# Token tiles in shared PSUM banks, and the low parts of the samples made by VectorE, in a hybrid decoder layer

## The chip, the cores and the metric

The kernel runs on one core of a Trainium2 chip. The metric is device time in microseconds (us) of one execution. Before the change it took 1491.72 us, the median of 3 runs (1490.73 to 1493.11).

In the profile PE is TensorE (matmuls), PEld its weight loads, DVE is VectorE, ACT is ScalarE, POOL is GpSimd, and SP (SyncE) issues the DMAs. L554 is line 554 of the kernel's file.

## The reference, cut to what matters

One inference step of a one-layer decoder, for a prompt of 1024 tokens and for 64 sample tokens (8 sequences of 8) that share the weights. The change touches the first stage only: the norm of the tokens, and the columns v and gmlp_v of the first projection.

```python
def rmsnorm(x, g):
    y = x * rsqrt(mean(x * x, axis=-1, keepdims=True) + EPS)
    return y * g

h = rmsnorm(x, norm_mix)                           # (tokens, 1024)
q, k, v, gu, gv, ga, gb = split_in(h @ w_in)
o = attention(q, k, v)                             # window of 128, per-head sinks
vn = layernorm(gelu(gv), ln_g, ln_b)
s = gelu(gu) * (tril(w_s) @ vn + b_s)              # inside chunks of 128 positions
merged = sigmoid(ga) * (o @ w_pa) + sigmoid(gb) * (s @ w_pb)
x = x + merged @ w_out
x = x + conv_ffn(rmsnorm(x, norm_ffn))             # up, conv of width 3, gelu gate, down
y = rmsnorm(x, norm_final)
```

All is in float32. The kernel splits each float32 factor into a high part (a rounding that TensorE multiplies in one pass) and a low part (what is left), and adds three products: high by high, high by low and low by high.

## The kernel before, in words

**Tiling of the first stage.** The tokens are in two groups. Group 0 has 576: the 64 samples ("s") and four tiles of 128 prompt tokens. Group 1 has four tiles of 128. The 1024 channels are 8 chunks of 128, numbered k. For v and gmlp_v the tokens are the stationary operand and 256 columns of weights the moving one, so that one token tile takes 8 chunks by 3 products = 24 matmuls of 128x256, and the sample tile 16: its high and low parts stand side by side in one array of 128 columns (`both` in `h_of`), so that high and low are multiplied by one matmul with the high weights and one with the low.

**The start.** For each chunk k of group 0 the tile `x` is loaded, and `h_of` makes the parts: ACT the high part of all 576 tokens (L536), DVE the low part of the 512 prompt tokens (L538, one scalar-tensor-tensor), and POOL the low part of the 64 samples in two instructions (L542, L543) by way of a tile `hx`. PE multiplies the chunk as it comes into five accumulators (`ps5`, one PSUM bank for each token tile; L554 is the matmul of `mm_tok`). Between these, ACT squares each chunk in place (L648), DVE adds the eight squares up (`rsg[0]`, L650, 128x576 each), and the weights are split too (L40 and L41; `w2h`, `w2l`). `stats_tok` (L494 to L501) then sums the squares over the channels on PE (tile `mx`), and ACT and DVE make 1/rms of it (`rst`). No accumulator can be taken out before that, since each is scaled by `rst`.

**The token sets.** `tokens(g, key, out, ...)` runs one set: all token tiles of a group by 256 columns. The sets are, in order: gv 1, v, gv 2 on group 0 (5 tiles each); v, gv 2, gv 0, gv 1 on group 1 (4 tiles each). gv 0 on group 0 is the start above. Each tile's matmuls go into a bank of its own, from the pool `psa` of seven (tag `st`). `out` takes it out: ACT scales it by `rst` (L569 for v, L596 with the gelu for gv), for the samples after ACT has copied one half of the partitions (L561) and DVE has added the other (L562, tile `gs`). In between, ACT and DVE also do jobs for group 1: its x (L44, L45, L665 to L668), and sums of the T0 tiles.

**What sets the order.** Each engine works through its instructions strictly in the order of a table, `ORDER`, by which `issue_order` rearranges what the code above emits. Semaphores between engines, and waits for a buffer that is to be used again, are put in by the framework.

Of the kernel before, what the change touches and what calls it, by code (L numbers as in the profile page):

```python
# [6 lines left out]
F32 = mybir.dt.float32  # L7
# [3 lines left out]
ALU = mybir.AluOpType  # L11
# [23 lines left out]
def layer(tc, a):  # L35
    nc = tc.nc
    V, S, G, PE = nc.vector, nc.scalar, nc.gpsimd, nc.tensor
# [5 lines left out]
    def scale_split(hi, lo, src, by):  # L43
        S.activation(hi, src, AF.Copy, scale=by)  # L44
        V.scalar_tensor_tensor(lo, src, by, hi.bitcast(F32), ALU.mult, ALU.subtract)  # L45

    with ExitStack() as top:
# [209 lines left out]
        def right(stack, name, bufs=1):  # L257
            return stack.enter_context(tc.tile_pool(name=name, bufs=bufs, side="right", reuse_waits="tile"))
# [122 lines left out]
        with ExitStack() as ph1:  # L381
# [109 lines left out]
            def bank():  # L491
                return psa.tile([P, 512], F32, name="st")
# [28 lines left out]
            hp0 = right(hs0o, "hs0")  # L521
# [3 lines left out]
            def h_of(g, k, x):  # L525
                n = groups[g]["n"]
                by = gains[:, 0, k:k + 1]
                if g:
                    hh, hl = (hp1.tile([P, n], F32R, name=f"h{y}{k}") for y in "hl")
                    scale_split(hh, hl, x, by)  # L530
                    hs[g].append((hh, hl, None))
                    return
                both = hp0.tile([P, 2 * n], F32R, name=f"h{k}")
                hh, hl = both[:, n:], both[:, 0:n - NS]
                for lo, hi in ((0, 320), (320, n)) if k == 0 else ((0, n),):
                    S.activation(hh[:, lo:hi], x[:, lo:hi], AF.Copy, scale=by)  # L536
# [493 lines left out]
            def acc2():  # L1030
                return pmm.tile([P, 1024], F32, name="mm")
# [420 lines left out]
            hx = {}  # L1452
# [247 lines left out]
        with ExitStack() as ph3:  # L1700
# [109 lines left out]
            bank = [psd.tile([P, 512], F32, name="dn") for _ in range(6)]  # L1810
# [90 lines left out]
def issue_order(tc):  # L1901
# [8 lines left out]
    for name, text in ORDER.items():  # L1910
# [14 lines left out]
DIGITS = "0123456789abcdefghijklmnopqrstuvwxyzABCDEFGHIJKLMNOPQRSTUVWXYZ"  # L1925
ORDER = {
    "Pool": (
        "(67)66(7)22..24..6(4)2..24..6(4)2..24..6(4)2..2(8)24..4..4..4..4..4..4..4..4..4..4..4..4(14)ff(4"
        ")1..11.2(4)22(4)2213.2..1(5)6d3..2...3..2...63.b.2...3..2...63..2.8a..3..2..21(4)7.3..2...63.b.2"
        "...3..2...63.b.2...3..2...3.b4.52..2(5)3.4.2.8..3..2...63.b.2...3..2...63.b.2...3..2...6..533.2."  # L1930
        "21"
# [17 lines left out]
        ".3.3(9)2j2i4.35e1466a.9.88.71(8)11121..14l13514g62.466aaaaa.91.1.1...1(5)1(5)1...1.1...1"  # L1949
    ),  # L1950
    "DVE": (
        "..nn2(6)91..1.44..2.1...1.1(6)123..3(4)1..1.1.1..26.1.31.2..2g.ff2.dd1ck.jj.iii...777cc.bd.c.b2a"
        ".9388.87.62.222(4)2.2.33.22g.1(6)e.e.cccficc(6)66a(5)3.5.235f..3.e45..4..468.1.51..3..192.23.7.3"
        "5..5.1(5)15..35[126]6[125][130]2[129]5.37h[130]..[138]5[136].g8[124](4)46(4)2449..26f.h...66(4)4"
        "47..49.3h.6i.9(5)46(4)2449..26fi(4)66(4)447..47.3d.4e.51..24..254e55555yyyy.4w4v.24dg22.2.1..249"
        "6b.1..22.13c3.d..2..2496b.31..1213.7a22..32546.3a.3b.2.13.6274a..47il..58...7.9.e.9.b..1b.ka.9.."
        "1h.7.8(4)6b8d(4)68hk(4)46..6.7.98.7..5.94.3..7.5..1423.23.11.1.3522.4723341.1(4)11(6)L1..227(4)4"
        "...11112.11122(6)1111...2x(4)22(4)J3.21.211.222..1.2N..11(4)2.221.11.2522..11N3312121.2..11(4)2R"
        "..11.11.2(4)22..222..1.2F..112.1.2.22(10)2.1.222...e.11...q(6)F(4)2(4)4332..151M33112.1333...161"
        "54T1..262143...1..3227..1..322N..151.32..1.4.22O..262.43...11433...1..222t..26254(4)151438h111.1"  # L1960
        "1(4)1b.22d.11...2.b...23e2.9.3..714.73.5.b4..55b.44..587..3..5.1.4.1.3.5...2.2413..31.131.2.3.7."
        ".d..633.1.14..2..11.3.1.33552262x24.22...u.25.16.244..3(5)12.2.24578957672755234.344757496.88871"
        "365..11(4)2262c5c.a3f9..g.6..46(4)2g5g..ddim...aa(4)8..6.f..6..aa.f9i..7...46(4)2g5g..ddim...aa("
        "4)8..6.f..6..aa.f9i..7...46(4)2g5g..ddhj...aa...8.7..4.4.2.7..5..3.2(5)11.4.e3.cc1h.aaah(4)8..6."
        "f..6..aa.f9i...6..46(4)2g5g..ddim...aa(4)8..6.f..6..aa.f9i..7...46(4)2g5g..ddim...aa(4)8..6.f..6"
        "..aa.e9f...6.5..4.3...1b.bag.9..7.6..6.5.2.14.a3ca..7.6ae.5.6(4)25fg..ddim...aa(4)8..6.f..6..aa."
        "f9i..7...46(4)2g5g..ddim...aa(4)8..6.f..6..aa.f9i..7...46(4)2g5g..ddim...aa(4)8..6.b..6..66.55.."
        ".b2a..1133.3.2(6)1322.1..7..4..2.1.1(8)1(4)51.1(9)1..11.11.11.11.11...11.a.8..1.4.[75]3.1..11.[6"
        "7][69].[68][70]..11.[65](7)7(6)2b.b.b8..1..6(5)23.3.3.3.3.3.b.b.b8b(5)3(4)23.3.3.3(9)88.7...77.1"
        "2...11.1..3..11..11(10)21311111...88(4)4a4...a..118.111.11.111...41.1.2(5)2..3.32..1"  # L1970
    ),
    "SP": (
        "(6)1(17)6789(4)7...3.2.a.ach(10)7.e.d.3d.c.1o(5)99.aa...948..625(4)33.23f.e..511(7)1(13)21.5(4)1"
# [109 lines left out]
```

## Time and profile before

| what | value |
|---|---|
| median of 3 runs | 1491.72 us |
| the profiled execution's own time | 1490.81 us |
| its span in the profile | 1489.1 us |
| PE busy in the span | 1480.2 us (99%) |
| DVE, ACT, POOL busy | 1181.0, 856.9, 286.6 us |
| granted TensorE clock, mean | 0.999 |
| matmuls of the first stage (L554) | up to 107.2 us of the span |
| share of the chain that ended last that is PE | 93% |

The span runs from the first to the last instruction; 1.7 us of the execution's time lie around it. A matmul's duration overlaps the next one's, so that where PE is fed, the starts are closer than the durations are long. Idle time is given for an engine before an instruction, with what released it.

### The profile page before, as it was taken

The numbers are of one execution on the slowest core, as the hardware profiler recorded it, in microseconds if no ns is written. First come the engines' busy times: TensorE is split into PE (matmuls) and PEld (weight loads), VectorE is DVE, ScalarE is ACT, GpSimd is POOL, SyncE is SP. The second block draws the span as 40 slices with busy tenths as digits, with TensorE's granted clock in tenths as the row PEclk, the third lists the DMA queues.
The fourth block names the chain that finished last, engine by engine and source line by source line (L and its number), as shares of the span: only waits on it lengthen the run. The fifth ranks groups of instructions, "written<-read, shape, count | busy, mean of one in ns | idle before, by whom it ended". The sixth has DMA issues, their size and how long they took to land.

```text
span 1489.1 us, 30035 instructions
## 1 busy us (share of the span) xinstructions
PE 1480.2 (99%) x11476; PEld 1445.6 (97%) x11476; DVE 1181.0 (79%) x1890; ACT 856.9 (58%) x1794; POOL 286.6 (19%) x392
## 2 busy tenths in 40 slices
PE   9999999999999999999999999999999999999998
PEld 9999999999998999998989999999999999999997
DVE  7888877655576887989578898898898888685586
ACT  8657776564465775864444554654565556363463
POOL 3002000010030222310234222332242222000002
PEclk9999999999999999999999999999999999999999
DMA  8687546764679757458977433332332316983354
GB/s 258 228 290 248 168 167 217 239 227 161 230 261 300 221 165 247 140 185 310 336 272 271 131 123 118 125 124 96 117 134 96 110 59 234 330 300 104 112 163 155
DMA packets 133791, 289.29 MB, mean 194 GB/s; under 512 B 15760, under 2 KB 35984, under 8 KB 133648
## 3 DMA queue, kind: packets, MB, share of 16 engines
q1 hardware_dynamic: 133504, 287.37, 57.6%
q8 instruction: 90, 1.47, 0.4%
q14 instruction: 53, 0.43, 0.1%
q10 hardware_dynamic: 144, 0.01, 0.0%
HBM read 198.77 MB, written 90.52 MB: 194 GB/s over the span
## 4 chain that ended last, share of the span: by engine, by line
PE 93%; DMA 2%; DVE 2%; issue 1%; ACT 1%; SPq 0%; POOL 0%; POOLq 0%; DVEq 0%; ACTq 0%
PE st L315 52%; PE mm L240 17%; PE dn L1725 11%; PE st L554 6%; PE sc L1221 2%; PE po L1272 2%; PE pt L1248 1%; DMA traw<-td 1%; DMA wraw<-wt 1%; PE mx L849 1%; DVE tl L41 1%; DVE wl L41 0%; DMA x<-xt 0%; PE po L1175 0%; ACT th L40 0%
## 5 line engine op out<-in xcount | busy, mean ns | idle before, releaser
L315 PE MATMUL st<-t,wh 128*128 128x288 f32 x2128 | 427.6, 294 | 0.0
L315 PEld LDWEIGHTS st<-t,wh 128*128 128x128 f32 x2128 | 335.6, 188 | 0.2
L315 PE MATMUL st<-t,wl 128*128 128x288 f32 x1064 | 311.8, 293 | 0.0
L315 PE MATMUL st<-th,wh 128*128 128x256 f32 x1064 | 294.6, 277 | 0.0
L315 PE MATMUL st<-tl,wh 128*128 128x256 f32 x1064 | 294.2, 277 | 0.0
L315 PE MATMUL st<-th,wl 128*128 128x256 f32 x1064 | 293.9, 276 | 0.0
L315 PEld LDWEIGHTS st<-th,wh 128*128 128x128 f32 x1064 | 199.8, 188 | 0.2 <-ACT kn L296 0.2
L315 PEld LDWEIGHTS st<-t,wl 128*128 128x128 f32 x1064 | 199.7, 188 | 0.0
L315 PEld LDWEIGHTS st<-th,wl 128*128 128x128 f32 x1064 | 199.7, 188 | 0.0
L315 PEld LDWEIGHTS st<-tl,wh 128*128 128x128 f32 x1064 | 199.7, 188 | 0.0
L40 ACT CAST wh<-wraw 128x512 fp32r<-128x512 f32 (+2 forms) x188 | 129.2, 700 | 87.4 <-DMA wraw<-wt 28.0
L1725 PE MATMUL dn<-th,wh 128*128 128x288 f32 (+1 forms) x616 | 176.8, 287 | 0.1
L1725 PE MATMUL dn<-tl,wh 128*128 128x288 f32 (+1 forms) x616 | 176.2, 286 | 0.0
L1725 PE MATMUL dn<-th,wl 128*128 128x288 f32 (+1 forms) x616 | 175.3, 285 | 0.0
L41 DVE TENSOR_TENSOR wl<-wraw,wh 128x512 fp32r<-128x512 f32 (+2 forms) x188 | 148.6, 804 | 26.4 <-ACT wh L40 24.4
L40 ACT CAST wh<-ws 128x512 fp32r<-128x512 f32 x168 | 102.7, 621 | 87.0 <-PE st L315 53.2
L41 DVE TENSOR_TENSOR wl<-ws,wh 128x512 fp32r<-128x512 f32 x168 | 117.5, 709 | 42.5 <-ACT wh L40 41.8
L1725 PEld LDWEIGHTS dn<-th,wh 128*128 128x128 f32 x616 | 115.6, 188 | 0.5 <-DVE x L1735 0.4
L1725 PEld LDWEIGHTS dn<-th,wl 128*128 128x128 f32 x616 | 115.9, 188 | 0.1
L1725 PEld LDWEIGHTS dn<-tl,wh 128*128 128x128 f32 x616 | 115.6, 188 | 0.1
L41 DVE TENSOR_TENSOR tl<-traw,th 128x544 fp32r<-128x544 f32 (+1 forms) x85 | 61.1, 723 | 21.1 <-ACT th L40 20.9
L40 ACT CAST th<-traw 128x544 fp32r<-128x544 f32 (+1 forms) x85 | 54.5, 642 | 38.2 <-PE dn L1725 29.2
(292 smaller groups left out, 3187.2 us busy)
## 6 DMA issues: line engine op xcount, KB each, us to landing
wraw<-wt SPq DMA_DIRECT2D x137, 512.0 KB
traw<-td SPq DMA_DIRECT2D x77, 272.0 KB
td<-za SPq DMA_DIRECT2D x22, 544.0 KB
q<-qd SPq DMA_DIRECT2D x16, 512.0 KB
upd<-hl SPq DMA_DIRECT2D x14, 512.0 KB
td<-t SPq DMA_DIRECT2D x11, 544.0 KB
wpart<-wt SPq DMA_DIRECT2D x22, 256.0 KB
qd<-q SPq DMA_DIRECT2D x8, 576.0 KB
```

The lines of the kernel that those rows point to most:

```text
L40: S.copy(hi, src)
L41: V.tensor_sub(lo, src, hi.bitcast(F32))
L240: PE.matmul(ps[:, lo:lo + c1 - c0], u[:, k, :], v[:, c0:c1], start=(k == 0 and i == 0), stop=(k == nk - 1 and i == 2))
L315: PE.matmul(ps, u[:, kk, :], v, start=first and kk + i == 0, stop=kk == 3 and i == 2, skip_group_check=True)
L554: PE.matmul(ps, u, v[:, k, :], start=k + i == 0, stop=k == KD - 1 and i == len(todo) - 1)
L849: PE.matmul(ps[:, P * i:P * i + P], vn[:, i], late["wst"][:, c, :], start=True, stop=True)
L1221: PE.matmul(ps[:, h, o0:256], q, kst[kv][:, e, k0:cur + P], start=e == 0, stop=e == 1)
L1248: PE.transpose(pt[:, h * P:h * P + P], s[:, h, 0:P], ident)
L1272: PE.matmul(po, v[:, kv, :], t, start=e == 0, stop=last)
L1725: PE.matmul(place(m, e), u[:, m, :], v[:, lo:hi], start=new and i + k == 0 and (e == 0 or m % 2 == 0), stop=i == NU - 1 and k == 2, skip_g ...
```

## The change

Three things are changed.

- In `h_of`, the low part of the samples is one scalar-tensor-tensor of DVE on 128x64, in place of two POOL instructions. The tile `hx` goes. There are 8 of these, one for each chunk.
- In `tokens`, the third tile of a set is written into the second half of the first tile's bank, and the fourth tile into the second half of the second's. A fifth tile has a bank of its own. So a set takes 3 banks (group 0) or 2 (group 1), not 5 or 4.
- The order table of DVE puts each new instruction behind the chunk's L538, and moves the sums of squares back. The table of POOL loses the 16 entries. Those of ACT, PE and SP are as they were.

```diff
@@ h_of
                     if not lo:
-                        t = hp0.tile([P, NS], F32, name="hx", bufs=2)
-                        G.tensor_scalar_mul(t, x[:, 0:NS], by)
-                        G.tensor_sub(both[:, n - NS:n], t, hh[:, 0:NS].bitcast(F32))
+                        V.scalar_tensor_tensor(both[:, n - NS:n], x[:, 0:NS], by, hh[:, 0:NS].bitcast(F32),
+                                               ALU.mult, ALU.subtract)
@@ tokens
+                banks = []
                 for i, (_, lo) in enumerate(groups[g]["toks"]):
-                    ps = bank()[:, :256]
+                    if i in (0, 1, 4):
+                        banks.append(bank())
+                    ps = banks[(0, 1, 0, 1, 2)[i]][:, 256 * (i in (2, 3)):][:, :256]
                     for k in range(KD):
                         mm_tok(ps, g, lo, wide[key], k)
@@ ORDER
     "Pool": (
-        "(67)66(7)22..24..6(4)2..24..6(4)2..24..6(4)2..2(8)24..4..4..4..4..4..4..4..4..4..4..4..4(14)ff(4"
+        "(51)66(7)22..24..6(4)2..24..6(4)2..24..6(4)2..2(8)24..4..4..4..4..4..4..4..4..4..4..4..4(14)ff(4"
     "DVE": (
-        "..nn2(6)91..1.44..2.1...1.1(6)123..3(4)1..1.1.1..26.1.31.2..2g.ff2.dd1ck.jj.iii...777cc.bd.c.b2a"
+        "..vv2(9)2(4)2..6(4)22.1(4)1.1(6)123..3(4)1..1.1.1..26.1.31.2..2g.ff2.dd1ck.jj.iii...777cc.bd.c.b"
```

**DVE, chunks 2 to 5 of the start, before.** `h` is a chunk's array of parts, `x` the chunk, `w2l` the low part of a weight tile, `rs` the sum of squares.

```order
L538 SCALAR_TENSOR_TENSOR h_340<-x_264,c_gains,h_340 128x512
L650 TENSOR_TENSOR rs_250<-x_262,x_263 128x576
L41 TENSOR_TENSOR w2l<-wraw,w2h 128x512
L538 SCALAR_TENSOR_TENSOR h_360<-x_265,c_gains,h_360 128x512
L538 SCALAR_TENSOR_TENSOR h_382<-x_266,c_gains,h_382 128x512
L41 TENSOR_TENSOR w2l<-wraw,w2h 128x512
L538 SCALAR_TENSOR_TENSOR h_402<-x_267,c_gains,h_402 128x512
L650 TENSOR_TENSOR rs_250<-rs_250,x_264 128x576
L650 TENSOR_TENSOR rs_250<-rs_250,x_265 128x576
L538 SCALAR_TENSOR_TENSOR h_424<-x_268,c_gains,h_424 128x512
```

The same place after the change:

```order
L538 SCALAR_TENSOR_TENSOR h_336<-x_264,c_gains,h_336 128x512
L541 SCALAR_TENSOR_TENSOR h_336<-x_264,c_gains,h_336 128x64
L41 TENSOR_TENSOR w2l<-wraw,w2h 128x512
L538 SCALAR_TENSOR_TENSOR h_354<-x_265,c_gains,h_354 128x512
L541 SCALAR_TENSOR_TENSOR h_354<-x_265,c_gains,h_354 128x64
L538 SCALAR_TENSOR_TENSOR h_374<-x_266,c_gains,h_374 128x512
L541 SCALAR_TENSOR_TENSOR h_374<-x_266,c_gains,h_374 128x64
L41 TENSOR_TENSOR w2l<-wraw,w2h 128x512
L538 SCALAR_TENSOR_TENSOR h_392<-x_267,c_gains,h_392 128x512
L541 SCALAR_TENSOR_TENSOR h_392<-x_267,c_gains,h_392 128x64
L652 TENSOR_TENSOR rs_250<-x_262,x_263 128x576
L538 SCALAR_TENSOR_TENSOR h_412<-x_268,c_gains,h_412 128x512
```

The first sum of squares has moved from behind chunk 2 to behind chunk 5, and the other six come behind chunk 6 or 7; a small instruction stands behind each L538.

**PE, from the second to the third tile of the set gv 1 on group 0, before.** `st_579` and `st_616` are the banks of these tiles, and what a matmul waits for stands in brackets.

```order
L554 MATMUL st_579<-w2h_470,h7_444 128x256
L554 MATMUL st_579<-w2l_471,h7_444 128x256
L554 MATMUL st_579<-w2h_470,h7_444 128x256
L554 MATMUL st_616<-w2h_470,h0_296 128x256 [waits Activation_49]
L554 MATMUL st_616<-w2l_471,h0_296 128x256
L554 MATMUL st_616<-w2h_470,h0_296 128x256
```

After the change, where `st_563` is the second tile's bank and `st_501` the sample tile's:

```order
L553 MATMUL st_563<-w2h_454,h7_430 128x256
L553 MATMUL st_563<-w2l_455,h7_430 128x256
L553 MATMUL st_563<-w2h_454,h7_430 128x256
L553 MATMUL st_501<-w2h_454,h0_296 128x256 [waits DVE_49]
L553 MATMUL st_501<-w2l_455,h0_296 128x256
L553 MATMUL st_501<-w2h_454,h0_296 128x256
```

Before, the third tile's first matmul waited until ACT had taken out an accumulator of the start, whose bank it takes over. Now it waits for DVE, which reads the sample tile out of the other half of the same bank (L562, L561 after the change).

## Rows read from the trace of the kernel before

**Rows 1.** The page: busy us, share of the span, instructions.
```profile
PE 1480.2 (99%) x11476; PEld 1445.6 (97%) x11476; DVE 1181.0 (79%) x1890; ACT 856.9 (58%) x1794; POOL 286.6 (19%) x392
```

**Rows 2.** Waits of PE, whole span: us in total, times, longest.
```profile
PE st L620 <- DVE c_ones L67: 1.2, 1, 1.2
PE fs L1770 <- DVE rt L1762: 0.6, 1, 0.6
PE st L554 <- DVE h L538: 0.2, 1, 0.2
```

**Rows 3.** Busy time by stretch: PE, PEld, DVE, ACT, POOL, clock, DMA share, GB/s.
```profile
10.00:20.00 10.00, 9.97 (x82) 9.74 (x82) 9.90 (x14) 9.86 (x15) 9.58 (x11) 1.00 1.02 348
24.00:34.00 10.00, 10.00 (x89) 10.00 (x89) 8.93 (x19) 9.46 (x20) 0.00 (x0) 1.00 0.65 190
```

**Rows 4.** Timeline of DVE: start, us, instruction, count, idle before and releaser.
```profile
6.34 0.48 DVE L538 SCALAR_TENSOR_TENSOR h<-x,c_gains,h 128x256 fp32r<-128x256 f32 x1 [0.68 <-ACT h L536]
8.52 0.76 DVE L41 TENSOR_TENSOR w2l<-wraw,w2h 128x512 fp32r<-128x512 f32 x1 [0.33 <-ACT w2h L40]
...
9.88 0.88 DVE L650 TENSOR_TENSOR rs<-x,x 128x576 f32<-128x576 f32 x1
10.68 0.68 DVE L41 TENSOR_TENSOR w2l<-wraw,w2h 128x512 fp32r<-128x512 f32 x1
11.32 1.48 DVE L538 SCALAR_TENSOR_TENSOR h<-x,c_gains,h 128x512 fp32r<-128x512 f32 x2
...
21.01 1.61 DVE L650 TENSOR_TENSOR rs<-rs,x 128x576 f32<-128x576 f32 x2
...
27.56 0.75 DVE L562 TENSOR_TENSOR gs<-st,gs 64x256 f32<-64x256 f32 x2
...
31.01 0.75 DVE L45 SCALAR_TENSOR_TENSOR hl<-stg,c_gains,hh 128x512 fp32r<-128x512 f32 x1
...
55.05 0.41 DVE L562 TENSOR_TENSOR gs<-st,gs 64x256 f32<-64x256 f32 x1
```

**Rows 5.** The tile hx: count, duration in ns (min/median/max), first and last start.
```profile
L542 POOL TENSOR_SCALAR hx<-x,c_gains x8: 442/909/2002, 3.4 to 17.3; 128x64 f32<-128x64 f32 x8
L543 POOL TENSOR_TENSOR h<-hx,h x8: 514/583/816, 4.1 to 19.4; 128x64 fp32r<-128x64 f32 x8
```

**Rows 6.** Timeline of PE, at the sums and at starts of third and fourth tiles.
```profile
22.68 1.28 PE L499 MATMUL mx<-c_ones,rs 128*128 128x1 f32 x10
23.81 0.48 PE L554 MATMUL st<-w2h,h 128*128 128x256 f32 x2
...
26.30 0.39 PE L554 MATMUL st<-w2h,h 128*128 128x256 f32 x2
...
29.02 0.39 PE L554 MATMUL st<-w2h,h 128*128 128x256 f32 x2
...
41.71 0.39 PE L554 MATMUL st<-w2h,h 128*128 128x256 f32 x2
...
53.15 0.39 PE L554 MATMUL st<-w2h,h 128*128 128x256 f32 x2
...
67.86 0.28 PE L554 MATMUL st<-w2h,hh 128*128 128x256 f32 x1
```

**Rows 7.** Timeline of ACT in the first stage.
```profile
9.98 0.62 ACT L40 CAST w2h<-wraw 128x512 fp32r<-128x512 f32 x1 [0.24 <-DMA wraw<-wt]
...
31.00 0.47 ACT L596 ACTIVATE gv<-st,rst 128x256 f32<-128x256 f32 x1
...
33.95 0.47 ACT L596 ACTIVATE gv<-st,rst 128x256 f32<-128x256 f32 x1 [0.46 <-DMA gvds<-gv]
...
43.95 0.47 ACT L569 ACTIVATE gv<-st,rst 128x256 f32<-128x256 f32 x1
...
61.63 0.47 ACT L596 ACTIVATE gv<-st,rst 128x256 f32<-128x256 f32 x1 [2.25 <-PE st L554]
...
67.48 0.48 ACT L569 ACTIVATE gv<-st,rst 128x256 f32<-128x256 f32 x1
```

More of the change, by code (lines that the diff above doesn't have):

```diff
@@ L1951 @@
     "DVE": (
-        "..nn2(6)91..1.44..2.1...1.1(6)123..3(4)1..1.1.1..26.1.31.2..2g.ff2.dd1ck.jj.iii...777cc.bd.c.b2a"
[L1953 to L1970, printed above, removed]
+        "..vv2(9)2(4)2..6(4)22.1(4)1.1(6)123..3(4)1..1.1.1..26.1.31.2..2g.ff2.dd1ck.jj.iii...777cc.bd.c.b"
@@ new lines @@
+        "2a.9388.87.62.222(4)2.2.33.22g.1(6)e.e.cccficc(6)66a(5)3.5.235f..3.e45..4..468.1.51..3..192.23.7"
+        ".35..5.1(5)15..35[126]6[125][130]2[129]5.37h[130]..[138]5[136].g8[124](4)46(4)2449..26f.h...66(4"
+        ")447..49.3h.6i.9(5)46(4)2449..26fi(4)66(4)447..47.3d.4e.51..24..254e55555yyyy.4w4v.24dg22.2.1..2"
+        "496b.1..22.13c3.d..2..2496b.31..1213.7a22..32546.3a.3b.2.13.6274a..47il..58...7.9.e.9.b..1b.ka.9"
+        "..1h.7.8(4)6b8d(4)68hk(4)46..6.7.98.7..5.94.3..7.5..1423.23.11.1.3522.4723341.1(4)11(6)L1..227(4"
@@ new lines @@
+        ")4...11112.11122(6)1111...2x(4)22(4)J3.21.211.222..1.2N..11(4)2.221.11.2522..11N3312121.2..11(4)"
+        "2R..11.11.2(4)22..222..1.2F..112.1.2.22(10)2.1.222...e.11...q(6)F(4)2(4)4332..151M33112.1333...1"
+        "6154T1..262143...1..3227..1..322N..151.32..1.4.22O..262.43...11433...1..222t..26254(4)151438h111"
+        ".11(4)1b.22d.11...2.b...23e2.9.3..714.73.5.b4..55b.44..587..3..5.1.4.1.3.5...2.2413..31.131.2.3."
+        "7..d..633.1.14..2..11.3.1.33552262x24.22...u.25.16.244..3(5)12.2.24578957672755234.344757496.888"
@@ new lines @@
+        "71365..11(4)2262c5c.a3f9..g.6..46(4)2g5g..ddim...aa(4)8..6.f..6..aa.f9i..7...46(4)2g5g..ddim...a"
+        "a(4)8..6.f..6..aa.f9i..7...46(4)2g5g..ddhj...aa...8.7..4.4.2.7..5..3.2(5)11.4.e3.cc1h.aaah(4)8.."
+        "6.f..6..aa.f9i...6..46(4)2g5g..ddim...aa(4)8..6.f..6..aa.f9i..7...46(4)2g5g..ddim...aa(4)8..6.f."
+        ".6..aa.e9f...6.5..4.3...1b.bag.9..7.6..6.5.2.14.a3ca..7.6ae.5.6(4)25fg..ddim...aa(4)8..6.f..6..a"
+        "a.f9i..7...46(4)2g5g..ddim...aa(4)8..6.f..6..aa.f9i..7...46(4)2g5g..ddim...aa(4)8..6.b..6..66.55"
@@ L1971 @@
+        "...b2a..1133.3.2(6)1322.1..7..4..2.1.1(8)1(4)51.1(9)1..11.11.11.11.11...11.a.8..1.4.[75]3.1..11."
+        "[67][69].[68][70]..11.[65](7)7(6)2b.b.b8..1..6(5)23.3.3.3.3.3.b.b.b8b(5)3(4)23.3.3.3(9)88.7...77"
+        ".12...11.1..3..11..11(10)21311111...88(4)4a4...a..118.111.11.111...41.1.2(5)2..3.32..1"
     ),
```

## The prediction, made blind

> **What bounds the kernel now.** I read the page first: PE is busy for 1480.2 of 1489.1 us [rows 1]. The list of PE's waits then shows whether that is real feeding or a model's smoothing: in the whole span there are three, together 2.0 us, none longer than 1.2 [rows 2]. So PE never waits for a PSUM bank today, and from the second chunk on nothing later in the kernel has slack that could swallow a delay: what PE loses in the first stage, the end loses. The granted clock is 1.00 in the stage, its upper level of 2.4 GHz [rows 3]. The change touches the first 107 us, so I went through these by the timelines. Two things are to be seen. First, in the start DVE is the engine that sets the pace: 9.90 of 10 us busy between 10 and 20, with PE, ACT and POOL beside it [rows 3]; its last sum of squares ends at 21.01 + 1.61 = 22.62, and PE's sum over channels starts at 22.68 [rows 4, 6]. Second, after that ACT runs behind PE: it is 9.46 of 10 us busy between 24 and 34 [rows 3], and the second tile of gv 1, done by PE at 26.41, is read at 31.00 to 31.47 [rows 6, 7]. Seven banks hide that distance today.
>
> **POOL's 16 instructions go.** No engine waits for them in a way that ends last, so nothing is gained on PE directly. Whether DVE gets faster beside an idle POOL is bounded by rows: an add of 128x576 took 0.88 us at 9.88 with POOL at work, and two took 1.61 at 21.01 without it [rows 4], so 0.08 each, for the five adds that stand in POOL's time 0.4 at most; a scalar-tensor-tensor of 128x512 took 0.74 at 11.32 and 0.75 at 31.01 [rows 4], no gain. I take 0.25, between 0 and 0.4.
>
> **Eight small instructions on DVE, and the sums moved (term A).** The trace has no 128x64 one on DVE. From 0.48 us for 256 columns and 0.74 for 512 [rows 4], 64 columns take about 0.285 (my estimate); instructions overlap by some 0.08, since the one at 10.68 starts 0.80 after one of 0.88 [rows 4]. So 0.2 in the queue, with 0.1 and 0.285 as ends. Chunks 0 and 1 fall into gaps of 0.68 and 0.33 [rows 4] and cost nothing. Behind chunk 2 stood the first sum of squares. It was nearly free there: the split behind it needs ACT's cast, which ends at 9.98 + 0.62 = 10.60 [rows 7], and it started at 10.68. Now that sum stands later, in the dense part, and costs 0.80 less the 0.05 given back; chunks 3 to 7 add 5 x 0.2 = 1.0. With the relief from POOL: 0.75 + 1.0 - 0.25 = 1.5 us, between 0.9 and 2.2. All of it lies ahead of the last sum, so PE's sum over channels starts at about 24.2. On the way PE may already wait a part of this for the low weights of gv 1, which stand behind the same instructions; that is one loss, not two. What follows on ACT (the square root, then all reads of the accumulators) is late by the same 1.5.
>
> **Tiles share banks (terms B to F).** The order of PE shows that the third tile's first matmul waits for DVE, the reader of the sample tile in the other half of the bank; the fourth waits likewise for ACT's read of the second. Since the tile between takes 2.72 us (29.13 less 26.41, the second matmuls of the pairs at 29.02 and 26.30 [rows 6]), a read has to end within that time. Queued behind the waiting matmul is all the rest of PE.
>
> - B, gv 1, third tile: wanted at 26.41; the reads of two sample tiles on DVE, the second of them this set's, end at 27.56 + 0.75 = 28.31 [rows 4]. Both move with A. Loss 1.9, and 0.1 for the first matmul after a stop (the pair at 23.81 took 0.48, one in the stream 0.39 [rows 6]): 2.0, between 1.7 and 2.2. The read can't come sooner, as ACT ahead of it is full.
> - C, gv 1, fourth tile: wanted at 26.41 + 2.0 + 2.72 = 31.13, read of the second ends at 31.47 [rows 7]: 0.4 with the restart, between 0.1 and 0.6.
> - D, v on group 0, fourth tile: wanted at 41.83 [rows 6] and PE is 3.9 late by now, so 45.73. The read ends at 43.95 + 0.47 = 44.42 [rows 7] and ACT's own lateness. That is A, and what ACT waits for the late fourth tile of gv 1: it comes at 29.13 + 2.4 + 2.72 + 0.17 = 34.42 where ACT read it at 33.95 [rows 7], so 0.47 more, 1.97 in all. 46.39 against 45.73: 0.7. At the ends, 0.2 if ACT's waits for loads take up the 0.47, and 2.4 if ACT is as late as PE.
> - E, gv 2 on group 0, third tile: wanted at 53.27 + 4.6 = 57.9, read at 55.05 to 55.46 and DVE's lateness [rows 4, 6]. At D's 2.0 that is 57.5, no wait; if DVE is as late as PE, 2.2. I take 0.
> - F, v on group 1, third tile: wanted at 67.86, read until 67.48 + 0.48 = 67.96 [rows 6, 7]. By here ACT waits for PE (2.25 us at 61.63 [rows 7]) and so is as late as PE; the 0.1 by which the read is later and the restart give 0.2, between 0 and 0.8. For the three sets after that I take nothing.
>
> The banks that come free give nothing back, since no matmul waits for one [rows 2].
>
> The Trainium skill (PSUM — Partial Sum Buffer, on bank collisions) says that two engines must not be in one bank and the same partitions at once, even at different columns, and that semaphores guard by bank, not by address. By that the waits of B to F can't be left out; without them the sum would be A alone. The skill's Perfetto Trace Analysis (Matmuls) also tells to let independent groups of matmuls rotate through different banks, so that taking one out overlaps the next; the trace of before does just that.
>
> **The sum.** A 1.5 + B 2.0 + C 0.4 + D 0.7 + E 0 + F 0.2 = 4.8 us. The profiled execution took 1490.81 us, 1.7 more than its span; with 4.8 it is 1495.6. The median of the three runs is 0.9 above that execution, so I predict 1491.7 + 4.8 = 1496.5.
>
> **Rivals.**
>
> - *Not slower: the reads end in time.* One mechanism, at the third tile of gv 1: ACT and DVE take the sample tile out before 26.41 + A. It decides at 1.9 us: so much earlier, against the sums, the read would have to be, for instance because the order by engine leaves room that the row does not show. Then only A is left, 1493.2. For it: the same waits on DVE and ACT exist today and none shows on PE [rows 2]. Against it: ACT is full there [rows 3].
> - *POOL was in DVE's way.* If DVE stood while POOL read, up to 8 x 0.58 = 4.7 us of POOL's second instructions [rows 5] would come back to DVE; A goes to nothing, and 1495.0 is left. Against: 0.74 and 0.75 with and without POOL, above. The Trainium skill (SBUF — State Buffer, Who interferes with whom) has the rule behind this: a VectorE instruction with two SBUF inputs and a GpSimd one that reads SBUF exclude each other for the whole instruction. By it 1495.0 is the time; the rows agree in POOL, whose hx took 442 to 2002 ns [rows 5], hardly in DVE.
> - *Every return waits.* If ACT stays as far behind in all seven sets, each loses what B loses: 1.5 + 7 x 2.0 = 15.5, 1507.2. Against: ACT waits for PE by 61.63 [rows 7].
> - *Faster.* No row holds 3 us to gain: PE's waits are 2.0 in all [rows 2].
>
> **How the numbers follow.** Forecast 0.68, reads in time 0.13, POOL in the way 0.10, every return 0.07, faster 0.02. The range goes from 1493.2, the first rival's time, to 1500.0: A and D at their upper ends (2.2, 2.4), with C and F at theirs (0.6, 0.8), give 1499.7. About 0.2% (3 us, so 1488.7 and 1494.7) is what a measurement of this kernel tells from no change. Slower by more: the forecast but for its lowest part (0.65), half of POOL in the way (0.06), every return (0.07): 0.78. Same: 0.20. Faster: 0.02.
>
> **What would show it.** In the profile after: PE's list of waits gains the last sum of squares (about 1.5 us with the wait for the low weights), the add of the sample halves (about 2.0) and ACT's reads for v and gv (about 1.3 together); the add of the halves ends near 29.8; POOL is idle in the first 25 us; the first matmul of L315 starts near 112 instead of 107.2; from there on the two traces run in parallel. I am wrong if the third tile of gv 1 starts without a wait, if the sums end before 23.5, or if L315 starts less than 3 us later.

## The result, and the profile after

The change made the kernel 0.3% slower: 1496.36 us (median of 9 runs, 1495.51 to 1498.64) against 1491.72 (9 runs, 1490.71 to 1494.23), ratio 1.0031 with a 95% interval of 1.0023 to 1.0040. The profiled execution took 1495.51 us, its span is 1493.8; before these were 1490.81 and 1489.1, so there are 4.7 us to be found between the two traces.

First the page's busy times and PE's waits of the kernel after (us in total, times, longest); they answer to [rows 1, 2].

```profile
PE 1482.3 (99%) x11476; PEld 1447.9 (97%) x11476; DVE 1182.3 (79%) x1898; ACT 857.4 (57%) x1794; POOL 276.5 (19%) x376
```

```profile
PE st L553 <- DVE gs L561: 1.7, 1, 1.7
PE st L622 <- DVE c_ones L67: 1.2, 1, 1.2
PE mx L499 <- DVE rs L652: 1.0, 1, 1.0
PE fs L1772 <- DVE rt L1764: 0.6, 1, 0.6
PE st L553 <- DVE h L538: 0.3, 1, 0.3
PE st L553 <- ACT gv L595: 0.2, 1, 0.2
```

Three waits are new: for the add of the sample halves (`gs`, 1.7), for the last sum of squares (`rs`, 1.0) and for ACT's read of the second tile (`gv`, 0.2). PE's timeline of the kernel after places them (start, us, instruction, then idle before it and its releaser); it answers to [rows 6]:

```profile
23.73 1.28 PE L499 MATMUL mx<-c_ones,rs 128*128 128x1 f32 x10 [1.02 <-DVE rs L652]
24.87 0.48 PE L553 MATMUL st<-w2h,h 128*128 128x256 f32 x2
...
29.42 0.39 PE L553 MATMUL st<-w2h,h 128*128 128x256 f32 x1 [1.72 <-DVE gs L561]
...
32.59 0.39 PE L553 MATMUL st<-w2h,h 128*128 128x256 f32 x1 [0.16 <-ACT gv L595]
```

The sum over channels starts at 23.73 instead of 22.68. The first matmul of the third tile of gv 1, the second half of the pair at 26.30 before, starts at 29.42, behind the add of the halves, which ends at 28.62 + 0.75 = 29.37 in DVE's timeline of the kernel after (against [rows 4]):

```profile
10.20 0.28 DVE L541 SCALAR_TENSOR_TENSOR h<-x,c_gains,h 128x64 fp32r<-128x64 f32 x1
...
14.48 0.75 DVE L652 TENSOR_TENSOR rs<-x,x 128x576 f32<-128x576 f32 x1
...
21.27 2.41 DVE L652 TENSOR_TENSOR rs<-rs,x 128x576 f32<-128x576 f32 x3
...
28.62 0.75 DVE L561 TENSOR_TENSOR gs<-st,gs 64x256 f32<-64x256 f32 x2
```

A small instruction lasts 0.28 us and takes 0.20 in the queue; an add of 576 columns lasts 0.75 where it lasted 0.88 beside POOL. Last, two pieces of each trace's chain that ended last (start, us, what), of before and then of after. They are the last three sets of group 1 (288 matmuls) and the work of L315 behind them; a piece begins a little behind the start of its first matmul:

```profile
74.57 32.66 PE st L554 x288
107.23 221.35 PE st L315 x1788
```

```profile
78.39 33.93 PE st L553 x288
112.32 221.36 PE st L315 x1788
```

The 288 matmuls took 1.27 us longer without any wait among them: 117.8 ns from start to start instead of 113.4. From L315 on the traces run in parallel. Where PE lost its time, by the start of the same matmul in both traces:

| matmul | before, us | after later by | share | term |
|---|---|---|---|---|
| sum over channels | 22.68 | 1.05 | 1.05 | A |
| gv 1, third tile | 26.41 | 3.01 | 1.96 | B |
| gv 1, fourth tile | 29.13 | 3.46 | 0.45 | C |
| gv 1, fifth tile | 31.85 | 3.59 | 0.13 | none: the restart behind C's stop |
| v on group 0, fourth tile | 41.83 | 3.59 | 0 | D |
| gv 2 on group 0, third tile | 53.27 | 3.59 | 0 | E |
| gv 2 on group 0, fifth tile | 58.71 | 3.77 | 0.18 | none: the return at the fourth tile |
| v on group 1, third tile | 67.86 | 3.91 | 0.14 | F |
| start of the last three sets | 74.33 | 3.82 | -0.09 | none |
| first of L315 | 107.07 | 5.09 | 1.27 | none |

The last share is negative because the matmuls of after are the faster ones there (see "The pace"). Behind 1313 us 0.37 come back, 0.28 of it at one matmul that before started late (1313.96); 4.7 are left.

### The profile page after: what moved, and what is told of

Same layout as the page of the kernel before. It is cut to its first block, busy times and chain, and to the rows that moved or that the text cites. A ratio compares the mean times of both kernels' runs of the same rounds, so it can differ in the third digit from the quotient of the medians.

```text
span 1493.8 us, 30013 instructions
## 1 busy us (share of the span) xinstructions
PE 1482.3 (99%) x11476; PEld 1447.9 (97%) x11476; DVE 1182.3 (79%) x1898; ACT 857.4 (57%) x1794; POOL 276.5 (19%) x376
## 4 chain that ended last, share of the span: by engine, by line
PE 96%; ACT 1%; DVE 1%; issue 1%; DMA 0%; POOL 0%; POOLq 0%; SPq 0%; ACTq 0%; DVEq 0%
PE st L315 52%; PE mm L240 17%; PE dn L1727 15%; PE st L553 5%; PE sc L1223 2%; PE po L1274 2%; PE pt L1250 1%; PE mx L851 1%; DMA x<-xt 0%; PE po L1177 0%; DVE rs L652 0%; ACT gv L595 0%; POOL x L1803 0%; DVE h L538 0%; ACT x L650 0%
## 5 line engine op out<-in xcount | busy, mean ns | idle before, releaser
L315 PE MATMUL st<-t,wh 128*128 128x288 f32 x2128 | 427.6, 294 | 0.0
L315 PEld LDWEIGHTS st<-t,wh 128*128 128x128 f32 x2128 | 335.6, 188 | 0.2
L315 PE MATMUL st<-t,wl 128*128 128x288 f32 x1064 | 311.8, 293 | 0.0
L315 PE MATMUL st<-th,wh 128*128 128x256 f32 x1064 | 294.6, 277 | 0.0
L315 PE MATMUL st<-tl,wh 128*128 128x256 f32 x1064 | 294.2, 277 | 0.0
L315 PE MATMUL st<-th,wl 128*128 128x256 f32 x1064 | 293.9, 276 | 0.0
L315 PEld LDWEIGHTS st<-th,wh 128*128 128x128 f32 x1064 | 199.8, 188 | 0.2 <-ACT kn L296 0.2
L315 PEld LDWEIGHTS st<-th,wl 128*128 128x128 f32 x1064 | 199.8, 188 | 0.0
L315 PEld LDWEIGHTS st<-t,wl 128*128 128x128 f32 x1064 | 199.8, 188 | 0.0
L315 PEld LDWEIGHTS st<-tl,wh 128*128 128x128 f32 x1064 | 199.7, 188 | 0.0
```

Source lines behind the costliest of these rows:

```text
L315: PE.matmul(ps, u[:, kk, :], v, start=first and kk + i == 0, stop=kk == 3 and i == 2, skip_group_check=True)
```

## The experiments

**Each half of the change by itself.** In the table the median of each kernel stands beside that of the kernel before in the same job.

| kernel | median, us | before | later by | ratio, 95% interval |
|---|---|---|---|---|
| shared banks alone (e1) | 1495.29 | 1491.21 | 4.1 | 1.0023 (1.0013 to 1.0033) |
| low parts on DVE alone (e2) | 1493.31 | 1491.21 | 2.1 | 1.0014 (1.0005 to 1.0023) |
| after, banks come back one tile later (e3) | 1493.13 | 1491.21 | 1.9 | 1.0011 (1.0002 to 1.0019) |
| after, again (e7) | 1496.53 | 1491.92 | 4.6 | 1.0031 (1.0019 to 1.0043) |
| after with fillers (e5) | 1496.60 | 1491.92 | 4.7 | 1.0028 (1.0017 to 1.0039) |
| e2 with fillers (e6) | 1492.37 | 1491.92 | 0.5 | 1.0003 (0.9994 to 1.0012) |
| e1 with fillers (e11) | 1494.12 | 1491.34 | 2.8 | 1.0016 (1.0007 to 1.0025) |
| e3 with fillers (e12) | 1492.44 | 1491.34 | 1.1 | 1.0005 (0.9997 to 1.0014) |

e4, e9 and e10 ran once each, for their traces: 1499.42, 1494.72 and 1495.05 us; so did e8, the kernel before, 1491.19.

*e1, shared banks alone:* the kernel before with this edit.

```diff
+                banks = []
                 for i, (_, lo) in enumerate(groups[g]["toks"]):
-                    ps = bank()[:, :256]
+                    if i in (0, 1, 4):
+                        banks.append(bank())
+                    ps = banks[(0, 1, 0, 1, 2)[i]][:, 256 * (i in (2, 3)):][:, :256]
```

> The kernel before with the shared banks alone; the samples' low parts stay on POOL and DVE's order is that of before. My theory: the loss at the returns to a bank is DVE's and ACT's reads coming late, so the third tile of gv 1 starts 1.96 us later than before and the fourth 0.45 more (as after shows them, 26.41 to 28.4 and 29.13 to 31.5), the sum over channels starts at 22.7 as before; L315 starts near 109.7, the time is 2.4 us over before (ratio 1.0016), and 1.2 more if the matmuls between 78 and 112 us run at 118 ns instead of 113. Rival, 'late only because of the small instructions': with the sums in time the reads are in time too, third tile without a wait, L315 near 107.3, ratio 1.000. On the pace of matmuls, 117.8 instead of 113.3 ns apart between 78 and 112 us in the profile after: if two tiles in a bank cause it, this kernel shows it and the next one does not; if it is drawn anew after each stop of PE, either may show it.

The third tile came 1.96 later against the sums, the same size as in the kernel after, so the small instructions have no part in B. But the kernel lost more than the 2.4 expected: the fourth tile was 3.22 later than before, and then the fifth 3.68. Its timeline of PE at the third tile, and its busy time by stretch (us, PE's busy time and count, granted clock, DMA share, GB/s):

```profile
28.29 0.38 PE L554 MATMUL st<-w2h,h 128*128 128x256 f32 x1 [1.80 <-DVE gs L562]
```

```profile
28.00:30.00 2.00, 1.71 (x13) 0.95 0.82 197
30.00:32.00 2.00, 2.00 (x11) 0.50 0.72 238
32.00:34.00 2.00, 2.00 (x14) 0.69 0.69 198
34.00:36.00 2.00, 2.00 (x20) 1.00 0.51 138
```

After a stop of 1.80 us the granted clock fell to 0.50, its lower level of 1.2 GHz, from about 29.8 to 33. PE is called busy there, and does 11 matmuls in 2 us instead of 20. No step of my prediction had this.

*e2, low parts on DVE alone:* the kernel after with `ps = bank()[:, :256]` for each tile again.

> The kernel after with a bank for each tile again; the low parts stay on DVE and the sums behind them. My theory: only term A is left, the sum over channels starts at 23.7 (before 22.67), the third tile of gv 1 follows without a wait, L315 starts near 108.3, the time is 1.05 us over before (ratio 1.0007). The rival of two tiles in a bank as the cause of the slow pace: 113.3 ns between 78 and 112 us here. Rival 'the pace comes from where POOL's and DVE's work or the tiles in SBUF stand': 117.8 ns here, so 1.3 us more, L315 near 109.6.

The sum over channels started at 24.15, behind a stop of 1.01; the next tile, which has nothing to wait for, was 4.23 later than before. The clock again, in the same columns:

```profile
22.00:24.00 2.00, 1.14 (x9) 1.00 1.03 404
24.00:26.00 2.00, 1.85 (x11) 0.68 0.13 49
26.00:28.00 2.00, 2.00 (x10) 0.50 0.60 161
28.00:30.00 2.00, 2.00 (x11) 0.50 0.72 249
30.00:32.00 2.00, 2.00 (x13) 0.61 0.77 213
```

At L315 it was 4.67 later, so behind the stop, by which the sums were 1.5 late, another 3.2 us were lost in this execution, which is 1.7 longer than the median of e2. The pace of the last three sets was 113.4 ns (288 in 32.66).

*e3, the bank comes back one tile later:* the kernel after with this edit.

```diff
-                    if i in (0, 1, 4):
+                    if i in (0, 1, 2):
                         banks.append(bank())
-                    ps = banks[(0, 1, 0, 1, 2)[i]][:, 256 * (i in (2, 3)):][:, :256]
+                    ps = banks[(0, 1, 2, 0, 1)[i]][:, 256 * (i in (3, 4)):][:, :256]
```

> The kernel after, still with three banks a set, but the bank comes back one tile later: the fourth tile shares with the first, the fifth with the second. My theory, that what counts is the distance between a tile's end and the return to its bank: the fourth tile of gv 1 is wanted at 31.1 to 31.9 (third tile at 27.46 and 29.1 plus 2.72), the sample's read ends at 29.4, no wait; the fifth at 32.9, ACT's read of the second ends at 32.5, no wait or under 0.1. B and C go, A's 1.05 stays: L315 near 108.3, ratio 1.0007, plus 1.3 us if the slow pace falls between 78 and 112 us. Rival, 'any return to a used bank costs PE something' (a wait's handling, a half-used bank): loss of 0.1 to 0.4 at each of the 14 returns, so 1.5 to 5 us more, ratio 1.002 to 1.004.

No matmul waited at a return: from the third tile of gv 1 to L315 this kernel stays 2.81 behind before, within 0.01 at every tile. A bank used twice costs nothing by itself; it costs what its reader is late. Of the 2.81, 1.21 are A and 1.6 the clock, at 0.50 between 25 and 29.

**The clock.** The theory by now: a stop costs itself and, in some executions, a stretch at half the clock. (Behind the stop at the sums PE does ten matmuls of one column each, 1.1 us with little work as well.) To test it, PE gets work in the stops, matmuls of ones into columns of the bank of `mx` that nobody reads.

*e5, the kernel after with fillers:*

```diff
+                fill = [PE.matmul(mx[:, P:2 * P], ones, ones, start=True, stop=True).ins for _ in range(4)]
                 for i, (_, lo) in enumerate(groups[g]["toks"]):
                     PE.matmul(pt[:, i:i + 1], acc[:, lo:lo + P], ones[:, 0:1], start=True, stop=True)
...
+                    fill = [PE.matmul(late["mx"][:, P:2 * P], ones, ones, start=True, stop=True).ins
+                            for _ in range(7)] if key == ("gv", 0, 1) and i == 2 else []
```

> The kernel after, and PE does matmuls of ones that nobody reads while it would stand: 4 of 128x128 ahead of the sum over channels, 7 ahead of the third tile of gv 1 (about 0.22 us each, so 0.9 and 1.5 us in stops of 1.0 and 1.7 to 1.9). Theory 'a stop costs the clock too': in four of the five profiles with such a stop the granted clock falls to 0.50 within 0.1 to 1.6 us of its end and stays for 3 to 8 us; with PE at work there is no fall in this kernel's first 110 us, the waits' 3.6 us stay (third tile at 29.4, fourth at 32.6), L315 starts between 110.7 and 112.4 (the rest is the pace), the median is 1494.8 to 1496.1 and the highest of the runs no more than 2.5 over the lowest. Rival 'the fall has nothing to do with the stop': 0.50 shows in the stretch 24 to 34 as often as without fillers, and the median is that of the kernel after in the same job.

*e6, low parts on DVE alone (e2) with the four fillers:*

> The low parts on DVE with a bank for each tile, and 4 matmuls of ones on PE ahead of the sum over channels. Without them this kernel's median was 1493.31 (1492.31 to 1496.29), 2.1 over before, where the late sum alone makes 1.05. Theory 'a stop costs the clock too': no fall of the clock at 24 us, the third tile of gv 1 1.0 to 1.3 us later than before (27.4 to 27.7; 30.64 without fillers), L315 near 108.3 to 108.6, median 1492.3 to 1492.8, highest below 1494.5. Rival 'nothing to do with the stop': 0.50 after 24 us again, median 1493.3.

*e7, the kernel after as it is:*

> The kernel after as it is, beside the two with fillers. If the fall of the clock is drawn in each execution, this profile may have one (after the sum's wait near 24 or after the wait for the add near 30), and then its L315 starts 1 to 3 us later than the start of B's wait explains; median 1495.8 to 1496.4. If the pace of matmuls between 78 and 112 us is fixed by the program (two tiles of a set in two banks), it is 117.8 ns here again; if it is drawn anew after a stop, one in two.

*e8, the kernel before as it is:*

> The kernel before as it is, for a second look at its pace and clock. No stop over 0.5 us ahead of 112 us, so no fall of the clock; L315 starts at 107.2 plus up to 1.3 if the pace of 117.8 ns takes another stretch (78 to 112 us) than in the first look; 113.3 ns there if the program fixes it.

*e11, shared banks alone (e1) with the seven fillers of the third tile:*

> The shared banks alone, as in the kernel whose median was 4.1 us over before, and 7 matmuls of ones on PE ahead of the third tile of gv 1, in its stop of 1.8 us. Theory 'the stop costs B and the clock behind it': no granted clock of 0.50 between 29 and 34 us, the third tile 1.9 us later than before, the fourth 2.3 to 2.5 (3.2 with the fall), the fifth 2.4 to 2.6 (3.7); the median 2.6 to 3.6 over before. Rival 'the fall has nothing to do with the stop': median 4.1 over before, 0.50 shows.

*e12, the later return (e3) with the four fillers:*

> A mended form of the change: three banks a set that come back one tile later (fourth with first, fifth with second), low parts on DVE, and 4 matmuls of ones ahead of the sum over channels. Without the fillers this form's median was 1.9 us over before and its profile had the clock at 0.50 from 24.9 to 29 us. Theory: no fall, no wait at a return, only A is left: third tile 1.1 to 1.3 us later than before and all after it alike, but for the pace; L315 at 108.2 to 109.7; median 0.5 to 1.3 over before, so same as before within what can be measured. Rival 'a return costs by itself': over 2.

With fillers the granted clock was 1.00 in every stretch from 18 to 112 us in all four kernels. Two stretches where it had been 0.50, of e6 (against e2) and of e11 (against e1):

```profile
26.00:28.00 2.00, 2.00 (x20) 1.00 0.82 247
28.00:30.00 2.00, 2.00 (x20) 1.00 0.83 275
```

```profile
30.00:32.00 2.00, 1.85 (x16) 1.00 0.67 227
32.00:34.00 2.00, 2.00 (x19) 1.00 0.42 99
```

In e6 the third tile was 1.11 later than before, as A alone should have it, and the median came from 2.1 over before to 0.5; e11's fell from 4.1 to 2.8, with B at 1.95 and C at 0.44. (L315 started at 110.54 in e6, 1.9 behind the expectation's upper end, by the slow pace in most of the stage.) The rival "nothing to do with the stop" does not fit these two.

Over all 14 profiles: a stop of 1.0 us at the sums was followed by 0.50 in four of five (e2, e3, e4, e7, not in the first profile of after), a stop of 1.7 to 1.8 at the third tile in one of three (e1; not after, e10). The seven without such a stop at these places show no fall, though one of them, e9, has a stop of 1.33 at 21.67. The granted clocks of all executions agree: their mean was 0.9971 over the 46 executions of after, e1, e2, e3 and e7, 0.9981 over the 40 with fillers, and 0.9980 over the 64 of before in the same jobs. The Trainium skill (TensorE: Matmul & The Clock Gate, A second HAM failure mode: psum-queue depth-cycling) tells of a kernel in which short idle times of PE between groups of matmuls, as it cycles through PSUM banks, made the clock swing. e1 has one such idle time, 1.80 us at the return to a bank, and one fall to 0.50 behind it; no run here shows a swing that repeats.

For the kernel after, however, the fillers brought nothing: 4.7 over before with them, 4.6 without. Its second profile (e7) tells why. Stretch and timeline of PE:

```profile
26.00:28.00 2.00, 2.00 (x13) 0.54 0.58 153
28.00:30.00 2.00, 1.78 (x9) 0.60 0.93 321
```

```profile
29.87 0.39 PE L553 MATMUL st<-w2h,h 128*128 128x256 f32 x1 [0.22 <-DVE gs L561]
```

The clock did fall behind the sums, but PE only came to the third tile later and then waited 0.22 for the add instead of 1.72: the slow stretch lies in B's wait, and the third tile starts when the add ends either way. The two losses of the halves (4.1 and 2.1, against 4.6) don't add up, and my expectation that e5 would fall below after was wrong.

e5 shows something else that I had not expected. In the last sets one more return waited, in PE's timeline and then ACT's:

```profile
84.73 0.39 PE L558 MATMUL st<-w2h,hh 128*128 128x256 f32 x1 [1.00 <-ACT gv L602]
```

```profile
78.07 0.41 ACT L40 CAST vst<-gv 128x256 fp32r<-128x256 f32 x1 [2.55 <-DMA vd<-vst]
```

ACT stood 2.55 us for a transfer out of `vst` (0.45 in e7), its read of the first tile of gv 2 came late, and the third tile, which shares the bank, waited. With a bank for each tile no matmul would have waited for this read; that is argued, no run shows it. e11 had a small one at the same place (0.21 at 83.10).

**The pace.** It is not fixed by the program: in e8, the second profile of the kernel before, matmuls are 117.8 ns apart between 24 and 47 us, where the first has 113.3, and L315 is 0.77 later for that reason alone. Its last sets took 32.66 us again, while after had 33.93 in both profiles. The starts of the matmuls show where the pace turns (ns from start to start):

| profiles | v on group 1, first tile | second tile, behind the sums of group 1 | fourth tile, behind return F | last three sets |
|---|---|---|---|---|
| before, e2, e3, e8, e9, e12 | 113.3 | 117.8 | 117.8 | 113.3 |
| after, e1, e5, e7, e10, e11 | 113.3 | 117.8 | 113.3 | 117.8 |
| e6 | 117.8 | 113.3 | 113.3 | 117.8 |
| e4 | 117.8 | 113.3 | 117.8 | 117.8 |

e11 began the last sets at 117.8 and went on at 113.3 behind its stop at 83.10. The pace turned at the sums of group 1 in all 14 profiles, at the third tile of v on group 1 in the seven in which PE stops there for its bank and in none of the others, and at the eight small matmuls ahead of the last sets in 13 (not in e4). So return F, short as it is, turns the pace, and the last three sets then run at the other one: the 1.27 us go with the pairing of the change. e1, which adds this stop, has them and e3, which takes it away, has not, but nothing moved this stop alone. It is no rule for every place: at ten small matmuls near 47 us the pace turned in two of the 14, and e5's stop at 84.73 left it as it was. Why a stop turns it stays open.

**What POOL costs DVE.** *e4, the kernel after, with POOL's 16 instructions once more:*

```diff
                         V.scalar_tensor_tensor(both[:, n - NS:n], x[:, 0:NS], by, hh[:, 0:NS].bitcast(F32),
                                                ALU.mult, ALU.subtract)
+                        t = hp0.tile([P, NS], F32, name="hx", bufs=2)
+                        G.tensor_scalar_mul(t, x[:, 0:NS], by)
+                        u = hp0.tile([P, NS], F32, name="hy", bufs=2)
+                        G.tensor_sub(u, t, hh[:, 0:NS].bitcast(F32))
```

> The kernel after, and POOL makes the samples' low parts once more, into tiles that nobody reads. It tells what POOL's work costs DVE. My theory: an add of 128x576 on DVE lasts 0.75 us in the profile after where it lasted 0.88 beside POOL before, a split of 128x1024 1.22 against 1.34, so about 0.65 us over the stage; with POOL at work again the sum over channels starts near 24.4 instead of 23.73 and the adds of squares are back at 0.80 to 0.88. Rival, 'POOL is not in the way' (my prediction's 0.25, at most 0.4): 23.73 to 24.1. The rest as after: third tile of gv 1 0.65 us later, L315 near 113.

The sum over channels started at 24.52, 0.79 later than in after; the expectation said 0.65, the prediction had allowed 0.4. Rows of DVE in e4:

```profile
10.86 0.69 DVE L41 TENSOR_TENSOR w2l<-wraw,w2h 128x512 fp32r<-128x512 f32 x1 [0.54 <-ACT w2h L40]
...
12.21 0.35 DVE L541 SCALAR_TENSOR_TENSOR h<-x,c_gains,h 128x64 fp32r<-128x64 f32 x1
...
13.94 0.81 DVE L538 SCALAR_TENSOR_TENSOR h<-x,c_gains,h 128x512 fp32r<-128x512 f32 x1
...
14.93 0.74 DVE L656 TENSOR_TENSOR rs<-x,x 128x576 f32<-128x576 f32 x1
...
18.98 1.34 DVE L41 TENSOR_TENSOR w2l<-wraw,w2h 128x1024 fp32r<-128x1024 f32 x1
```

Not all of the 0.79 is POOL's. The split at 10.86 waited for ACT's cast, which waited for its load, and started 0.25 later than in after (10.61). From this split to the end of the last sum DVE took 13.60 us, in after 13.06: POOL costs 0.54, between the prediction's bound and my theory. In after the instructions at 12.21, 13.94 and 18.98 lasted 0.28, 0.75 and 1.22 us, so those that POOL lengthens last 0.06 to 0.12 more. It does not lengthen each one beside it: the add at 14.93 took 0.74, and the adds did not go back to 0.80 to 0.88 as expected. The clock fell behind the sums here too, so the third tile was 1.44 later than in after, not 0.65.

The same stretch, from that split to the end of the last sum, is 13.05 or 13.06 us in all seven profiles with the change's order of DVE and without POOL (after, e2, e3, e5, e6, e7, e12), and 11.89 to 11.97 in those with the order of before (before, e1, e8, e11). So A is 1.1; the split itself starts between 10.52 and 11.08, as its weights come, and that alone makes A 1.05 in after and 1.50 in e7.

**The two parts of A.** *e9, the kernel before with the sums of squares alone moved, and e10, the kernel after with them put back.* In the order of DVE (S1 to S7 are the adds, L and s the low parts of a chunk, W the splits of weights), e9:

```diff
-L2 S1 W L3 L4 W L5 S2 S3 L6 L7 S4 W S5 W S6 S7 W
+L2 W L3 L4 W L5 S1 L6 L7 S2 S3 W S4 W S5 S6 S7 W
```

and e10:

```diff
-L2 s2 W L3 s3 L4 s4 W L5 s5 S1 L6 s6 L7 s7 S2 S3 W S4 W S5 S6 S7 W
+L2 s2 S1 W L3 s3 L4 s4 W L5 s5 S2 S3 L6 s6 L7 s7 S4 W S5 W S6 S7 W
```

> The kernel before with DVE's sums of squares alone moved to where the change puts them (the first behind chunk 5, the second and third behind chunk 7, the others each one place later); low parts on POOL, a bank for each tile. It tells term A's parts apart. My prediction's step: the first sum was nearly free behind chunk 2 and costs 0.75 us in the dense part, so the sum over channels starts at 23.4 instead of 22.68. Rival, from the profile after, in which DVE has no gap between 10.6 and 25 either way: the order alone changes nothing but which work is late, 22.7 to 22.9.

> The kernel after with the sums of squares put back to the places they had before; small instructions and shared banks stay. If the two parts of A simply add (0.75 for the move, the rest for the small instructions), the sum over channels starts at 23.73 - 0.75 = 22.98. Rival: with the small instructions there the gap behind chunk 2 is only 0.13 us (DVE's small one ends at 10.48, the split starts at 10.61), so putting the sum back gains 0.1 to 0.2: 23.5 to 23.6, and the weights behind it come 0.5 later.

In e10 the sum over channels started at 23.11, so the move costs 0.62 of A's 1.05 and the small instructions, less what POOL gives back, 0.43. My prediction's 0.75 was near, and the expectation's rival (23.5 to 23.6) is out. The rows of DVE show why the first sum is nearly free behind chunk 2 even there:

```profile
9.98 0.75 DVE L652 TENSOR_TENSOR rs<-x,x 128x576 f32<-128x576 f32 x1
10.71 0.69 DVE L41 TENSOR_TENSOR w2l<-wraw,w2h 128x512 fp32r<-128x512 f32 x1
```

The split behind it starts at 10.71, and at 10.61 in after without the sum.

In e9 the sum over channels started at 24.14, 1.46 later than before, and two things beside the move are in that. Timelines of POOL and PE in e9:

```profile
18.50 2.00 POOL L542 TENSOR_SCALAR hx<-x,c_gains 128x64 f32<-128x64 f32 x1
20.58 1.04 POOL L543 TENSOR_TENSOR h<-hx,h 128x64 fp32r<-128x64 f32 x1
```

```profile
21.67 0.38 PE L554 MATMUL st<-w2h,h 128*128 128x256 f32 x1 [1.33 <-POOL h L543]
```

Beside DVE's splits and adds POOL took 2.00 and 1.04 us for the last chunk, and PE waited 1.33 for the sample's low part; so it came to the sums 0.25 behind DVE, whose last one ended at 23.89. And the split behind chunk 2 started at 11.04, 0.36 later than before. From it to the end of the last sum DVE took 12.85 us instead of 11.95: beside POOL the move costs 0.9, in e10 without POOL 0.62, and the rival of 22.7 to 22.9 is out here too. The Trainium skill (SBUF — State Buffer, Who interferes with whom) has VectorE's second pair of ports shared with GpSimd under an exclusive lock. The trace agrees in kind: here POOL pays most (2.00 us at the worst, where such an instruction took 0.44 at the best), and DVE 0.54 in all in e4.

## Why the prediction was right, and where it was not

The time forecast was 1496.5, the median 1496.36. Step by step:

- **What bounds.** Right: nothing behind the first 112 us takes a loss up. L315's piece is 221.36 us long against 221.35. What the step did not see is that PE's pace and clock are not fixed: 113.3 and 117.8 ns at a granted 1.00, and a granted 0.50 behind stops that before does not have.
- **A, 1.5 forecast, 1.05 measured**, within its bounds. The move of the sums was sized well (0.75 against 0.62) and so was a small instruction (0.2 in the queue, as forecast). The term that was mis-sized is POOL's relief: 0.25, at most 0.4, against 0.54 (e4) to 0.57 (five small ones at 0.2, less the 0.43 of e10). I had bounded it by halves of merged rows. The pair of scalar-tensor-tensors at 11.32 in [rows 4], read as 0.74 each, is one of 0.75 and one of 0.81, which overlap; the two adds at 21.01, read as 0.80 each, last 0.75 and 0.76 with DVE idle for 0.1 between. So POOL cost an add 0.13 and not 0.08, and a scalar-tensor-tensor up to 0.06 and not nothing.
- **B, 2.0 forecast, 1.96 measured**: right in size and place, and the same to 0.01 in e1, e10 and e11, with and without A. The distance of the read from the sums is what counts.
- **C, 0.4 forecast, 0.45 measured**: right; 0.44 in e10 and in e11.
- **D, 0.7 forecast, nothing measured**, under the lower end of its bounds. The step that failed is ACT's lateness at the read for v's fourth tile, which I carried forward as 1.97 us. Up to the read ahead of it that was right: in ACT's timelines, of before and then of after, the read at 40.20 is at 42.16, 1.96 later. The read at 43.95 [rows 7] is at 44.57, only 0.62 later.

```profile
40.20 0.50 ACT L569 ACTIVATE gv<-gs,rst 64x256 f32<-64x256 f32 x1
40.97 0.73 ACT L44 ACTIVATE hh<-stg,c_gains 128x512 fp32r<-128x512 f32 x1 [0.27 <-DMA stg<-xt]
42.68 0.72 ACT L44 ACTIVATE hh<-stg,c_gains 128x512 fp32r<-128x512 f32 x1 [0.99 <-DMA stg<-xt]
```

```profile
42.16 0.49 ACT L568 ACTIVATE gv<-gs,rst 64x256 f32<-64x256 f32 x1
42.56 1.33 ACT L44 ACTIVATE hh<-stg,c_gains 128x512 fp32r<-128x512 f32 x2
...
44.57 0.48 ACT L568 ACTIVATE gv<-st,rst 128x256 f32<-128x256 f32 x1
```

  Between the two reads ACT had waited 0.27 and 0.99 us for loads; in after the loads were there, and its lateness went into these waits. The read ends at 45.05, and PE comes at 45.42. My lower bound had such waits take up 0.47; they took up 1.3. (The upper bound was off too: by its own rows, 44.42 less 41.83, it is 2.6 and not 2.4. The range would have held it.)
- **E, 0 forecast, 0 measured; F, 0.2 forecast, 0.14 measured**, 0.25 with the restart. In e1, E was 0.4: the read comes close there. The sum had no term for the fourth tile of gv 2 on group 0, whose return cost 0.18 in after: ACT had stood 1.53 us for a transfer and read the second tile until 59.57, just when PE came.
- **"For the three sets after that I take nothing."** This is the place of the error that hid the others: 1.27 us by the pace, which turns at return F. Without it the sum of waits, 3.8 at 74 us, would have come out 1.0 under the 4.8 forecast. That the time is right to 0.2 us is luck: two errors of opposite sign, A and D too large by 1.15, the pace missing. How much of the difference of medians is pace can't be said from spans alone, as before has slow stretches too (0.77 in e8).
- **The rivals.** "The reads end in time" is out: the third tile waited for the add in every kernel with the change's pairing. "POOL was in DVE's way" had the mechanism right and the size wrong, 0.54 to 0.57 of the 1.75 that it needs. "Every return waits" did not come as such, but e5 showed one of its returns waiting 1.0 in an execution with a late transfer. e3 and e12 tell what it hangs on: with the return one tile later no return waits.

Of what I named as signs, the waits for the last sum (1.0 instead of 1.5), the add (1.7 and the restart) and ACT's read of gv came, but ACT's reads made 0.2 in the list instead of 1.3, as none for v on group 0 waited; the add ended at 29.37 instead of 29.8, L315 started at 112.16 against "near 112".

A mended form, e12, keeps the low parts on DVE and three banks a set, with the return one tile later and four fillers. It is the same as before within what can be measured (1.0005, 0.9997 to 1.0014). No kernel here beats the one before; what A leaves, about 1.1, is DVE's work in a stretch of the start, from 10.6 us on, in which it has almost no gap (0.17 us of 13.06).

## What to carry to other kernels

When two tiles share a PSUM bank, count the distance from the end of a tile to the next write into its bank, and compare it with the time that its reader is behind PE; one tile more of distance took away every wait at a return here. A stop of PE on a path without slack has to be priced with the clock behind it, between nothing and three times its own length; a few matmuls into unused columns in the stop took that away. Two losses in a row on one engine don't add where the second is a wait for a fixed time: it swallows what the first adds.

## What the runs showed of the hardware that was not expected

- Matmuls of 128x256 in a row have two paces at a granted clock of 1.00: 113.3 and 117.8 ns from start to start. A pace lasts for a stretch (24 to 47 us in e8, 78 to 112 in after), differs between executions of the same program, and turned at stops and at small matmuls (at one place in all 14 profiles, at another in the seven that stop there). Over 288 matmuls it makes 1.27 us.
- The granted clock went to 0.50 behind stops of 1.0 and 1.8 us, in five of eight stops of that length at these two places, 0.6 us (e2, at 24.7) to 2.0 us (e7, at 26.2) after the stop's end, and stayed there for 3 to 7 us. Four or seven matmuls into unused columns during the stop kept it at 1.00 in four profiles of four.
- POOL's work beside DVE lengthened many, not all, of DVE's instructions by 0.06 to 0.13 us each (0.28 to 0.35, 0.75 to 0.81, 0.75 to 0.88, 1.22 to 1.34), 0.54 us over some 25 of them in e4. A POOL instruction of 128x64 that took 0.44 us elsewhere took 2.00 beside DVE's splits and adds (e9).
